# A two-layer decoder trunk: the down-projection of two SwiGLU blocks regrouped, with some additions moved from VectorE to GpSimd

## The chip, the cores and the metric

The kernel runs on one core of one Trainium2 chip. The metric is the device time of one execution in microseconds, as the median of several runs. Engines are named as in the profile: PE is TensorE (matmuls), PEld its weight loads, DVE is VectorE, ACT is ScalarE, POOL is GpSimd and SP is SyncE, which here only issues DMAs.

## What is computed

Two layers. Each layer adds half a SwiGLU to the residual, then a mixing part (attention beside a short convolution), then half of a second SwiGLU. There are therefore four SwiGLUs; the change touches the second (end of layer 0) and the third (start of layer 1) in all its parts, and the first and fourth in one.

```python
D_MODEL = 1024; SEQ = 512; DEPTH = 2; D_FF = 2816
def rms_norm(x, gain):
    inv = lax.rsqrt(jnp.mean(xf * xf, axis=-1, keepdims=True) + NORM_EPS)
    return (xf * inv).astype(x.dtype) * gain
def swiglu(h, w_gate, w_up, w_down):
    return (jax.nn.silu(h @ w_gate) * (h @ w_up)) @ w_down
for l in range(DEPTH):
    x = x + 0.5 * swiglu(rms_norm(x, ffn1_norm[l]), ffn1_wg[l], ffn1_wu[l], ffn1_wd[l])
    ...
    x = x + 0.5 * swiglu(rms_norm(x, ffn2_norm[l]), ffn2_wg[l], ffn2_wu[l], ffn2_wd[l])
return rms_norm(x, final_norm)
```

All data are float32. Every product is made of three matmuls: both factors are split into a rounded high part and a remainder (names ending in h and l), and high by high, high by low and low by high are added up in PSUM.

## The kernel before

The residual x stays in SBUF, features on partitions, as eight tiles of 128 x 512 (`xs[c]`, in pairs `xpair[m]`). The 2816 hidden columns of a SwiGLU are eleven blocks of 256, numbered 0 to 10. A table of stages gives the order of one SwiGLU (`INNER`, L33; `LAST`, L37, for the fourth). Its letters:

- **p**: gate and up of block 0, four groups of 24 matmuls. While they run, the norm's factor `inv` is found from the sum of squares (`factors`, L516, two matmuls in the second group), the normalized input is written in full (`scale`, L532, eight DVE operations named hf) and the first operand of the next stage is made (`make("b11")`).
- **d (0,)**: the part of the down-projection that belongs to block 0, 48 matmuls, added to x column by column (`down`, L343; L1249).
- **w b**: gate and up of blocks b and b+1 as a 2x2 block product with seven products in place of eight (Winograd's form), `winograd2`, L971. Each of the seven steps has two weight groups of 12 matmuls. The operands of the seven steps are b11, b21, t2, t3, t1, t4 and b22; t3 = b12 - b22, t2 = t3 - b11, t1 = b11 - b12 and t4 = t2 + b21 are sums of quarters of the input (`Seven.make`, L555), each 128 x 1024, and each operand is then split (ACT for the high part, DVE for the low part). They are made once, before and during the first w stage, and kept.
- **s b**: the down-projection of the four blocks from b on, again with seven products (`share`, L832), 168 matmuls. Its result is token-major; the `Apart` class keeps four quarters (o, t), sends them through DMA transposes (`send`, L892) and adds them to x (`back`, L902; one quarter goes through PE transposes).
- **d (9, 10)**: the part of blocks 9 and 10, 96 matmuls, with the last quarters added and, for each finished column c, `after(c)` (class `into`, L1672): the next norm's input split (`take`, L449: ACT and DVE) and the square added to the running sum nacc (`square`, L460: ACT, then a DVE addition at L467).
- **e 5** (fourth SwiGLU only): blocks 5 to 10 in one group with seven products of three weight groups each, 252 matmuls.

Weights come from HBM in pieces of 512 KB into eight buffers (`raw`); a sum of two weight blocks is made by a second, accumulating DMA that POOL issues (L220). Every weight group is then split into wh and wl (`need_split`, L233), three buffers of each, always two groups ahead of its use (`SPLIT_AHEAD`, L65). Normally ACT makes wh and DVE wl (L225). A group marked "far" spares DVE: ACT writes the negated weights to wl, and a DMA that POOL issues adds the raw weights to it (`split_far`, L227, L231). For a group marked "share" the sum of the weight blocks a12 and a11 is made by a DMA (L282) in place of a DVE addition (L284).

The framework orders each engine's instructions by their place in the program and by the buffers that come free, and sets the semaphores. Each engine, and each queue of DMA issues, then runs in that fixed order: an instruction that waits holds back those behind it.

Of the kernel before, what the change touches and what calls it, by code (L numbers as in the profile page):

```python
# [16 lines left out]
P = 128  # L17
# [19 lines left out]
LAST = INNER[:-2] + (("e", 5),)  # L37
FORMS = ("a11", "a12", "s2", "s3", "s1", "a22", "s4")
# [13 lines left out]
SENT_AT = {3: (0, 0), 4: (1, 1), 5: (1, 0)}  # L52
BACK_AT = {4: ((0, 0), (0, 1)), 5: ((1, 0),)}
# [21 lines left out]
def trunk_kernel(  # L75
# [29 lines left out]
    work = ctx.enter_context(tc.tile_pool(name="work", bufs=1))  # L105
    ps = ctx.enter_context(tc.tile_pool(name="ps", bufs=1, space=bass.MemoryType.PSUM))
# [126 lines left out]
    def need_split(g):  # L233
        while state["split"] <= min(g, len(order) - 1):
# [16 lines left out]
            elif isinstance(what, tuple):  # L251
# [4 lines left out]
                need_raw(u + h if far else u + max(last, 4) + h + LOAD_AHEAD)  # L256
# [33 lines left out]
            if far:  # L290

                with tc.issue_after(sent.ins):
                    need_raw(u + LOAD_AHEAD + (4 + h if isinstance(order[n][1], tuple) else 0))
# [62 lines left out]

    def plan():
# [19 lines left out]
        def ffn(wg, wu, wd, stages, near=False):  # L377
            for what, b in stages:
                how = "far" if b == (0,) and not near else None
                if what == "p":  # L380
                    plain(wg, wu, b)
                if what == "w":
                    seven(
                        lambda o, j, h: ((wg, wu)[o], KC // 2 * j + 2 * h, 2, 2 * b * P, S),
                        lambda what, h: "far" if (b, what, h) == (1, "a11", 0) else None,
# [6 lines left out]
                if what == "d":  # L392
                    cols(wd, 2 * b[0], 2 * len(b), KC, how, len(b) == 2)
# [14 lines left out]
        for l in range(DEPTH):  # L408
            ffn(ffn1_wg[l], ffn1_wu[l], ffn1_wd[l], INNER, l == 0)
# [7 lines left out]
            ffn(ffn2_wg[l], ffn2_wu[l], ffn2_wd[l], INNER if l + 1 < DEPTH else LAST)  # L417
# [18 lines left out]
    class Norm:  # L436
        def __init__(self, i):
# [5 lines left out]
            self.seven = Seven(self.full, room_g8, f"{i}")  # L443
# [16 lines left out]
        def square(self, c):  # L460
# [6 lines left out]
            nc.vector.tensor_add(self.acc, self.acc, sq)  # L467
# [78 lines left out]
    class Seven:  # L546
# [3 lines left out]
        def __init__(self, full, room, name, far=()):  # L550

            self.full, self.room, self.name, self.forms = full, room, name, {}
            self.far = far

        def make(self, *names):  # L555
            for what in names:
# [15 lines left out]
                if self.room is None:  # L572
# [7 lines left out]
                    if what == "t4":  # L580
                        nc.vector.tensor_add(b21, b11, b21)
# [295 lines left out]
    class Apart:  # L877
# [24 lines left out]
        def back(self, o, t):  # L902
# [824 lines left out]
```

## Time and profile before

| what | value |
|---|---|
| median of 3 runs | 1632.73 us (1632.26 to 1633.55) |
| the profiled execution | 1633.73 us, of which its span (first to last instruction) is 1631.9 us |
| PE matmuls | 7572, busy 1619.6 us |
| DVE, ACT, POOL busy | 1369.1, 1178.7, 223.5 us |
| read from HBM | 264.29 MB |

The profile is of one execution. Its parts are the busy time of each engine, the DMA queues, the chain of work that ended last (followed back from the last instruction), groups of instructions by line, and DMA issues. Further views of the same trace give the waits, the busy time of every engine in chosen stretches, and the instructions in order of time. A row of the timeline begins with its start and its length in us; consecutive matmuls overlap, so that their spacing, and not their length, is what each one costs. The second SwiGLU runs from 497 us to 820 us of the span, the third from 820 us to 1144 us.

### The profile page before, as it was taken

What the parts mean: (1) busy time and instruction counts of PE and PEld (TensorE: products, weight loads), DVE (VectorE), ACT (ScalarE), POOL (GpSimd) and SP (SyncE); (2) the same over time, 40 slices, a digit from 0 to 9 for tenths busy, and PEclk for the clock granted to TensorE, in tenths of its full rate; (3) what the DMA queues carried; (4) which work ended last, traced back from release to release, by engine and by line L of the source; (5) the groups of instructions that cost most, each with busy time, mean ns of one, the idle gap of its engine ahead of it and who ended that gap; (6) DMA issues with size and microseconds to landing.
All of it is one profiled execution on the core that took longest, in us unless ns stands there. A gap on an engine that the chain in (4) does not pass through costs nothing.

```text
span 1631.9 us, 21170 instructions
## 1 busy us (share of the span) xinstructions
PE 1619.6 (99%) x7572; PEld 1348.3 (83%) x7572; DVE 1369.1 (84%) x1779; ACT 1178.7 (72%) x1510; POOL 223.5 (14%) x199
## 2 busy tenths in 40 slices
PE   9999999999999999999999999999999999999998
PEld 6788888888898888888888888888888988888887
DVE  7978798888899877797998777979788998677997
ACT  6667778867766577777865777788586767878665
POOL 1211111001121111111011111110012111111121
PEclk9999999999999999999999999999999999999999
DMA  9899989922497699999966999999136978999992
GB/s 271 194 230 221 215 203 234 251 65 74 125 240 176 175 218 218 214 209 240 229 154 173 227 214 221 199 246 228 52 91 156 227 153 213 222 222 229 230 264 70
DMA packets 307166, 318.12 MB, mean 195 GB/s; under 512 B 125612, under 2 KB 188660, under 8 KB 307060
## 3 DMA queue, kind: packets, MB, share of 16 engines
q1 hardware_dynamic: 265140, 230.63, 49.9%
q0 software_dynamic: 41200, 85.47, 30.9%
q8 instruction: 59, 0.97, 0.2%
q10 hardware_dynamic: 720, 0.66, 0.1%
q14 instruction: 47, 0.39, 0.1%
HBM read 264.29 MB, written 2.10 MB: 163 GB/s over the span
## 4 chain that ended last, share of the span: by engine, by line
PE 89%; DVE 5%; ACT 3%; DMA 1%; issue 1%; SPq 0%; ACTq 0%; DVEq 0%
PE x L823 26%; PE y L823 13%; PE x_s L823 8%; PE w L823 6%; PE acc L311 6%; PE acc L312 6%; PE acc L314 6%; PE y_s L823 5%; PE x_m L808 3%; PE w_s L823 2%; PE y_m L808 1%; DVE wl L225 1%; PE y_e L823 1%; PE acc L685 1%; PE x_e L823 1%
## 5 line engine op out<-in xcount | busy, mean ns | idle before, releaser
L225 DVE TENSOR_TENSOR wl<-raw,wh 128x1024 fp32r<-128x1024 f32 (+1 forms) x493 | 598.4, 1221 | 172.6 <-ACT wh L225 171.7
L225 ACT CAST wh<-raw 128x1024 fp32r<-128x1024 f32 (+1 forms) x493 | 513.1, 1045 | 296.1 <-PE x L823 95.0
L311 PE MATMUL acc<-xh,wh 128*128 128x512 f32 x392 | 153.1, 392 | 0.5 <-ACT wh L225 0.5
L312 PE MATMUL acc<-xl,wh 128*128 128x512 f32 x392 | 153.4, 391 | 0.0
L314 PE MATMUL acc<-xh,wl 128*128 128x512 f32 x384 | 149.8, 390 | 0.0
L220 POOL DMA_DIRECT2D raw<-in_ffn_wu_dram x40 | 50.2, 1263 | 384.6 <-DMA raw<-in_ffn_wu_dram 311.2
L311 PEld LDWEIGHTS acc<-xh,wh 128*128 128x128 f32 x392 | 73.8, 188 | 15.1 <-ACT wh L225 0.6
L312 PEld LDWEIGHTS acc<-xl,wh 128*128 128x128 f32 x392 | 73.7, 188 | 15.0 <-DVE xl L458 0.5
L314 PEld LDWEIGHTS acc<-xh,wl 128*128 128x128 f32 x384 | 72.2, 188 | 15.0
L220 POOL DMA_DIRECT2D raw<-in_ffn_wg_dram x40 | 48.4, 1232 | 201.9 <-DMA raw<-in_ffn_wu_dram 104.7
L220 POOL DMA_DIRECT2D raw<-in_ffn_wd_dram x34 | 41.1, 1218 | 254.5 <-DMA raw<-in_ffn_wd_dram 99.9
L264 DVE TENSOR_TENSOR raw<-raw,raw 128x1024 f32<-128x1024 f32 x58 | 70.5, 1219 | 6.2 <-DMA raw<-in_ffn_wu_dram 4.7
L1085 ACT COPY raw_a<-turned 128x1024 uint16<-128x1024 uint16 x48 | 63.5, 1355 | 0.0
L823 PE MATMUL x<-wl,ft2h 128*128 128x512 f32 x160 | 62.2, 390 | 1.1 <-DVE wl L225 1.1
L823 PE MATMUL w<-wl,fb21h 128*128 128x512 f32 x160 | 62.4, 390 | 0.6 <-DVE wl L225 0.6
L823 PE MATMUL y<-wh,ft4h 128*128 128x512 f32 x160 | 62.4, 390 | 0.1
L823 PE MATMUL w<-wh,fb21h 128*128 128x512 f32 x160 | 62.4, 390 | 0.0
L823 PE MATMUL y<-wh,ft3h 128*128 128x512 f32 x160 | 62.3, 390 | 0.0
L823 PE MATMUL x<-wh,ft2h 128*128 128x512 f32 x160 | 62.3, 389 | 0.0
L823 PE MATMUL x<-wh,ft1h 128*128 128x512 f32 x160 | 62.3, 389 | 0.0
L823 PE MATMUL x<-wh,ft2l 128*128 128x512 f32 x160 | 62.3, 389 | 0.0
L823 PE MATMUL w<-wh,fb21l 128*128 128x512 f32 x160 | 62.3, 389 | 0.0
(506 smaller groups left out, 4544.2 us busy)
## 6 DMA issues: line engine op xcount, KB each, us to landing
raw<-in_ffn_wu_dram SPq DMA_DIRECT2D x127, 512.0 KB, 5.6
raw<-in_ffn_wd_dram SPq DMA_DIRECT2D x105, 512.0 KB, 5.7
raw<-in_ffn_wg_dram SPq DMA_DIRECT2D x86, 512.0 KB, 5.5
raw<-in_ffn_wu_dram POOLq DMA_DIRECT2D x40, 512.0 KB, 9.1
raw<-in_ffn_wg_dram POOLq DMA_DIRECT2D x40, 512.0 KB, 6.3
raw<-in_w_in_dram SPq DMA_DIRECT2D x36, 512.0 KB, 4.1
raw<-in_ffn_wd_dram POOLq DMA_DIRECT2D x34, 512.0 KB, 9.8
raw<-raw POOLq DMA_DIRECT2D x21, 512.0 KB, 8.2
```

The lines of the kernel that those rows point to most:

```text
L220: nc.gpsimd.dma_start(out=r, in_=rows_of(*more), accum_op=ALU.add)
L225: return nc.scalar.copy(hi, raw), eng.tensor_sub(lo, raw, f32(hi))
L264: nc.vector.tensor_add(a11, a11, s1)
L311: nc.tensor.matmul(acc, hi[:, k, :], rhs[k][0], start=k == first, stop=False)
L312: nc.tensor.matmul(acc, hi[:, k, :], rhs[k][1], start=False, stop=False)
L314: nc.tensor.matmul(acc, lo[:, k, :], rhs[k][0], start=False, stop=k == last)
L685: nc.tensor.matmul(opening[n], (lo if part == "w" else hi)[:, k, :], xl if part == "x" else xh, start=n not in begun, stop=k == KC - 1 and ...
L808: nc.tensor.matmul(accs[c // 2][:, c % 2, :], w[:, k, cols], x_[:, 2 * h + k, :], start=start and c % 2 == 0 and h + k + i == 0, stop=h + ...
L823: nc.tensor.matmul(accs[u], x_[:, 2 * h + k, tok], w[:, k, :], start=start and h + k + i == 0, stop=h + k == 2 and i == 2, skip_group_chec ...
L1085: nc.scalar.copy(words(raws[self.b][:, c, :]), self.to[:, :, c, :])
```

## The change

A new table of stages, `LATER`, takes the place of `INNER` for the second and third SwiGLU. In it:

- block 0's part of the down-projection moves from behind p to the very end. Its activation is not split at once; it is stored to DRAM by two DMAs on SP (`stay`), fetched back during the e stage (`bring`), and split there with the subtraction on GpSimd;
- w 1 follows p directly. Three of its first weight groups (a11 first half, a12 both halves) are "far", and the s3 sums are made by DMA; the operands are made two steps ahead of their use;
- s 5 and d (9, 10) become one e 5 group for blocks 5 to 10 (new function `six`), whose first operands are made during s 1. Two quarters of s 1's result are added to x in this stage, on GpSimd; the other two in the final d (0,).

In these two SwiGLUs the squares of the next norm are added on GpSimd. In all four SwiGLUs the sums t3, t2, t1 and t4 of the input are made on GpSimd (`adder`), and so are those of the e group in the second and third, but for t1.

```diff
+LATER = (
+    ("p", 0), ("w", 1), ("w", 3), ("w", 5), ("w", 7), ("w", 9), ("s", 1), ("e", 5), ("d", (0,)),
+)
+AHEAD = {4: ((0, ("b11",)),), 5: ((0, ("t2",)), (1, ("b11",))), 6: ((1, ("t2",)),)}
+SHARE_SENT_AT = {3: (1, 1), 4: (0, 0), 5: (1, 0)}
+SHARE_BACK_AT = {4: (1, 1), 6: (0, 0)}
+LATE_BACK_AT = {4: ((1, 0),), 5: ((0, 1),)}
+    away = ctx.enter_context(tc.tile_pool(name="away", bufs=1, space=bass.MemoryType.DRAM))
...
-                need_raw(u + h if far else u + max(last, 4) + h + LOAD_AHEAD)
+                need_raw(u + last + h if far else u + max(last, 4) + h + LOAD_AHEAD)
...
+    def first_how(what, h):
+        return {("a11", 0): "far", ("a12", 0): "far", ("a12", 1): "far"}.get(
+            (what, h), "share" if what == "s3" else None
+        )
...
         for l in range(DEPTH):
-            ffn(ffn1_wg[l], ffn1_wu[l], ffn1_wd[l], INNER, l == 0)
+            ffn(ffn1_wg[l], ffn1_wu[l], ffn1_wd[l], LATER if l else INNER, l == 0)
...
-            ffn(ffn2_wg[l], ffn2_wu[l], ffn2_wd[l], INNER if l + 1 < DEPTH else LAST)
+            ffn(ffn2_wg[l], ffn2_wu[l], ffn2_wd[l], LATER if l + 1 < DEPTH else LAST)
...
-            self.seven = Seven(self.full, room_g8, f"{i}")
+            self.seven = Seven(self.full, room_g8, f"{i}", adder=nc.gpsimd)
...
-            nc.vector.tensor_add(self.acc, self.acc, sq)
+            (nc.gpsimd if soft else nc.vector).tensor_add(self.acc, self.acc, sq)
...
                 if what == "t2":
                     self.sums = self.room(self.name)
                     t3, t2 = self.sums
-                    nc.vector.tensor_sub(t3, b12, b22)
-                    nc.vector.tensor_sub(t2, t3, b11)
+                    self.adder.tensor_sub(t3, b12, b22)
+                    self.adder.tensor_sub(t2, t3, b11)
                 if what == "t1":
-                    nc.vector.tensor_sub(b12, b11, b12)
+                    self.adder.tensor_sub(b12, b11, b12)
                 if what == "t4":
-                    nc.vector.tensor_add(self.sums[1], self.sums[1], b21)
+                    self.adder.tensor_add(self.sums[1], self.sums[1], b21)
...
+    def six(ops, accs, y, between):
+
+        for step, (acc, operand, (o, t, sign)) in enumerate(END):
+            start = acc not in accs
...
+            for n, op in enumerate(ops):
+                op.make(operand)
+                xh, xl = op.forms[operand]
+                for h in range(xh.shape[1] // 2):
+                    _, wh, wl = take_split()
+                    stream(accs[acc], wh, wl, xh, xl, h, start and n == 0)
+                if step + 1 < len(END):
+                    op.make(END[step + 1][1])
+            for u in range(2):
+                y.add(2 * t + u, o, accs[acc][u], 0.5 * sign)
+            between(step)
...
             def up(j, acc):
                 t = gates[j]
                 nc.vector.tensor_mul(t, acc, t)
-                split(hi[:, j, :], lo[:, j, :], t)
+                if delay:
+                    nc.sync.dma_start(out=stay[:, j, :], in_=t)
+                else:
+                    split(hi[:, j, :], lo[:, j, :], t)
...
                 norm.make("b11")
                 up(1, accs[3])
+                if delay:
+                    norm.make("b21")
...
-                if step < 3:
+                if delay and step < 5:
+                    norm.make(CHAINS[step + 2][1])
+                elif step < 3:
                     norm.make(CHAINS[step + 4][1])
...
+                def between(step):
+                    if step == 1:
+                        acts[0] = bring(acts[0])
+                    if step == 5:
+                        part = acts[0]
...
+                        split(hi, lo, part, nc.gpsimd)
+                    if step in SHARE_BACK_AT:
+                        apart.back(*SHARE_BACK_AT[step], nc.gpsimd)
+                    if step in SHARE_SENT_AT:
+                        apart.send(*SHARE_SENT_AT[step])
+
+                six(ends, kept, apart, between)
...
-                    for quarter in BACK_AT.get(c, ()):
+                    for quarter in (LATE_BACK_AT if delay else BACK_AT).get(c, ()):
...
-        ffn(norm, INNER, into(n1), None if l else bias_steps())
+        ffn(norm, LATER if l else INNER, into(n1, l > 0), None if l else bias_steps())
...
-            ffn(n2, INNER, into(n3))
+            ffn(n2, LATER, into(n3, True))
```

More of the change, by code (lines that the diff above doesn't have):

```diff
@@ L925, in back, with bring @@
                 nc.vector.tensor_add(part, part, tp)
+    def six(ops, accs, y, between):
+        for step, (acc, operand, (o, t, sign)) in enumerate(END):
+            start = acc not in accs
+            if start:
+                tag = {"x": "mm", "y": "sc", "w": "aux"}[acc]
+                accs[acc] = [psum(tag, [P, S], f"{acc}_{ops[0].name}_{u}") for u in range(2)]
+            for n, op in enumerate(ops):
[9 more added lines that the diff above has]
+            between(step)
+    def bring(stay):
+        part = form(f"near_{state['group']}", F32, (P, 2, S))
+        nc.sync.dma_start(out=part, in_=stay)
+        return part
     def ahead(ops, at):
@@ L1188, in ffn @@
                 winograd2(b, between)
-            if what == "s" and end:
+            if what == "s" and delay:
+                tail = crossing[-1]
+                ends = [
+                    Seven(lambda: [raws[5], raws[7]], None, f"e_{norm.i}_0", adder=nc.gpsimd),
+                    Seven(
+                        lambda: [tail.whole[:, j] for j in range(2)], None, f"e_{norm.i}_1", adder=nc.gpsimd
+                    ),
+                ]
+                share(
+                    ops,
+                    0.5,
+                    joined(lambda n: [ends[j].make(*what) for j, what in AHEAD.get(n, ())]),
+                    apart,
+                    still=kept,
+                )
+            elif what == "e" and delay:
+                def between(step):
[3 more added lines that the diff above has]
+                        part = acts[0]
+                        hi, lo = acts[0] = [
+                            form(f"a{n}_{norm.i}_0", shape=(P, 2, S)) for n in "hl"
+                        ]
+                        split(hi, lo, part, nc.gpsimd)
[4 more added lines that the diff above has]
+                six(ends, kept, apart, between)
+            elif what == "s" and end:
                 ends = [
```

48 lines of the change are left out of this document (29 added, 19 removed).

## The prediction

> **What bounds the kernel now.** The first part of the page and the sums of the chain that ended last say which engine sets the time:
>
> ```profile
> PE 1619.6 (99%) x7572; PEld 1348.3 (83%) x7572; DVE 1369.1 (84%) x1779; ACT 1178.7 (72%) x1510; POOL 223.5 (14%) x199
> PE 89%; DVE 5%; ACT 3%; DMA 1%; issue 1%; SPq 0%; ACTq 0%; DVEq 0%
> ```
>
> PE, without a break. What one matmul costs is read from the chain in order of time, where 24 matmuls make one step of a w stage; what PE waits for, from its waits over the whole span (the matmul rows among them):
>
> ```profile
> 612.10 5.44 PE w L823 x24
> 617.53 5.44 PE x L823 x24
> ...
> PE x L823 <- DVE wl L225: 1.1, 1, 1.1
> ...
> PE w L823 <- DVE wl L225: 0.6, 1, 0.6
> ```
>
> A step is 5.44 us, a matmul 5.44/24 = 0.227 us, and all the weights that came late cost 1.7 us. So the time is a count of matmuls plus a few stalls, and the question about any edit is whether PE still never waits. That hangs on the engine that feeds it, so next I read the busy times by stretch (columns: length; then busy us of PE, PEld, DVE, ACT, POOL; clock; DMA share; GB/s):
>
> ```profile
> 34.00:72.00 38.00, 36.87 (x161) 29.68 (x161) 37.72 (x39) 27.30 (x36) 10.35 (x11) 1.00 0.83 190
> 1317.00:1352.00 35.00, 35.00 (x160) 29.03 (x159) 34.40 (x41) 24.96 (x31) 5.44 (x5) 1.00 0.73 146
> 509.00:555.00 46.00, 46.00 (x205) 37.98 (x204) 45.11 (x52) 31.33 (x37) 7.54 (x7) 1.00 0.68 154
> 759.00:797.50 38.50, 38.37 (x168) 30.93 (x168) 35.52 (x37) 28.34 (x29) 4.20 (x4) 1.00 0.99 222
> 797.50:820.00 22.50, 22.50 (x105) 18.74 (x104) 21.04 (x31) 18.60 (x22) 0.00 (x0) 1.00 0.69 190
> 892.00:930.00 38.00, 38.00 (x169) 31.46 (x168) 27.61 (x29) 26.87 (x32) 5.42 (x5) 1.00 0.93 224
> ```
>
> In a plain w stage (892) DVE has 10 us of 38 free. In three kinds of stretch it has next to none: the openings of the SwiGLUs (34, 509, 1317: gates, normalized input, operands, w 1), s 5 (759), and the last stage d (9, 10) with the next norm's work (797.5). There PE is fed just in time. The change works on all of these.
>
> **The change, part by part.**
>
> *Fewer matmuls.* s 5 (168), d (9, 10) (96) become e 5 (252); p, w, s 1 and d (0,) keep theirs. 12 fewer in each of two SwiGLUs, 24 x 0.227 = **-5.4 us**. This part is certain, since PE is the bound in both stages.
>
> *s 5 against e 5.* In s 5 168 matmuls take 38.1 us and the stretch is 38.5: 0.4 us is lost there, twice. The e stage of the fourth SwiGLU shows what a group of this form costs:
>
> ```profile
> 1566.00:1624.00 58.00, 57.92 (x268) 47.99 (x267) 54.00 (x72) 34.37 (x49) 11.58 (x8) 1.00 0.54 129
> ```
>
> PE is busy throughout, with DMAs at 0.54, so the three more weight pieces (21 loads and sums in place of 18) are covered by free DMA time. If that cover were gone, three pieces at the stretch's 0.5 MB in about 2.4 us (222 GB/s above) would be 7 us, of which prefetch hides most. DVE is at 54 of 58, and GpSimd's own additions here (quarters, block 0's split) are new; I take 0.2 us lost in place of 0.4, **-0.4 us** for both (-0.8 to +4).
>
> *w 1 right behind p.* In the old order block 0's part, 11 us of PE, lay between p and w 1. These rows are the end of p and the preparation of a far group in the second SwiGLU (PE, ACT, POOL, DVE; then two far DMAs with their us to landing, and the summary of all of L231):
>
> ```profile
> 519.11 0.40 PE L314 MATMUL acc<-xh,wl 128*128 128x512 f32 x1
> 519.35 0.40 PE L330 MATMUL acc<-a,wh 128*128 128x512 f32 x1
> 519.54 1.06 ACT L229 ACTIVATE wl<-raw 128x1024 fp32r<-128x1024 f32 x1 [0.47 <-PE acc L314]
> 520.91 0.90 POOL L231 DMA_DIRECT2D wl<-raw  x1 [2.55 <-DVE a L225]
> 517.39 0.68 DVE L949 TENSOR_TENSOR gate<-acc,gate 128x512 f32<-128x512 f32 x1
> 517.99 1.22 DVE L225 TENSOR_TENSOR fb11l<-hf,fb11h 128x1024 fp32r<-128x1024 f32 x1
> ...
> wl<-raw POOLq DMA_DIRECT2D x1, 512.0 KB, 8.4
> wl<-raw POOLq DMA_DIRECT2D x1, 512.0 KB, 4.5
> DMA to landing us min/median/max: 4.4/7.7/9.1
> ```
>
> The buffer for a group comes free when the group three before it is done. At 519.35 p's last group ends, ACT negates until 520.6, the DMA is issued at 520.91, and lands 8.4 us later. In the old order that group is w 1's first, 10.9 us away: enough. In the new order the group in this very place is a12's first half, and only two groups of 12 lie before it: it is due at 519.35 + 5.44 + 0.45 (third matmul) = 525.2. With the median landing of 7.7 us it comes at 528.6, **3.4 us late**; with 4.5 (the other row, the first far copy during p) at 525.4, 0.2 late. At this place the row is 8.4, and w 1's other pieces are still loading in the new order too. I take 3.4. Queued behind this DMA on POOL are the second half's DMA and the sums t3 and t2; if a sum goes first, the DMA is later by up to 2.6 us, so 0.2 to 6. Beside it, fb11l ended at 519.2 for a PE that now needs it at 519.6. One more weight split (1.2 us) now stands before it on DVE and GpSimd's t3 runs beside it; up to 3 us, but the copy's clock starts at p's end, so this hides inside the 3.4. The two stores on SP hold back loads by at most an `up` multiplication (0.7 us), which eight buffers cover; the fetch back, one 512 KB DMA, has four e steps (over 30 us) before its use. Two SwiGLUs: **+6.8 us**.
>
> *Block 0's part last.* The old last stage, DVE operations from 797.7 to 827.1, and what waits for them at its end:
>
> ```profile
> L225 DVE TENSOR_TENSOR wl<-raw,wh 128x1024 fp32r<-128x1024 f32 x6 | 7.3, 1216 | 0.4 <-ACT wh L225 0.4
> L458 DVE SCALAR_TENSOR_TENSOR xl<-x,par,xh 128x512 fp32r<-128x512 f32 x8 | 5.9, 742 | 0.0
> L1249 DVE SCALAR_TENSOR_TENSOR x<-acc,x 128x512 f32<-128x512 f32 x8 | 5.3, 680 | 0.0
> L467 DVE TENSOR_TENSOR nacc<-nacc,nsq 128x512 f32<-128x512 f32 x7 | 4.8, 680 | 0.0
> L914 DVE TENSOR_TENSOR x<-x,back 128x512 f32<-128x512 f32 x6 | 4.0, 689 | 1.2 <-ACT back L910 1.2
> L890 DVE SCALAR_TENSOR_TENSOR apart<-x_s,apart 128x512 f32<-128x512 f32 x2 | 1.3, 680 | 0.0
> L925 DVE TENSOR_TENSOR x<-x,back 128x512 f32<-128x512 f32 x2 | 1.3, 678 | 0.0
> ...
> 825.00 0.68 DVE L467 TENSOR_TENSOR nacc<-nacc,nsq 128x512 f32<-128x512 f32 x1
> 826.37 0.69 DVE L225 TENSOR_TENSOR sql<-nacc,sqh 128x512 fp32r<-128x512 f32 x1 [0.69 <-ACT sqh L225]
> 827.17 0.39 PE L522 MATMUL ssq<-sqh,ones_r 128*128 128x512 f32 x1
> ```
>
> sql ends at 827.06 and PE takes the sum of squares at 827.17 and 227 ns later: no slack. The new last stage has half the matmuls. DVE must still do all evictions (8), input splits (8), apart additions (2), four of the eight quarter additions, and three weight splits: 5.3 + 5.9 + 1.3 + 1.3 + 1.3 + 3.7 = 18.8 us, less 0.08 us by which neighbours overlap, 26 times: 16.7, and about 1 us until the first group is done: 17.7. From the last split to sql the old order takes 2.1 us; with a GpSimd addition of 1.3 us (row below) in place of 0.68 it is 2.7, so 20.4 us from the stage's start. PE gets there after 48 + 24 + 6 matmuls and eight transposes (0.9 us): 18.6. **1.8 us late**, with no contention. The covers that go: the 10.9 us of matmuls under which this work lay. In return the squares (4.2 us) and two quarters leave DVE, counted above.
>
> *GpSimd's additions.* What such an addition takes, and what it does to DVE, from the convolution (POOL, then DVE):
>
> ```profile
> 403.84 1.29 POOL L1657 TENSOR_TENSOR cc<-cc,tap 128x511 f32<-128x511 f32 x1 [4.79 <-issue]
> 442.53 2.15 POOL L1658 TENSOR_TENSOR cc<-cc,inv 128x512 f32<-128x512 f32 x1
> 442.14 3.62 DVE L225 TENSOR_TENSOR wl<-raw,wh 128x1024 fp32r<-128x1024 f32 x2
> 405.21 1.64 POOL L1658 TENSOR_TENSOR cc<-cc,inv 128x512 f32<-128x512 f32 x1
> 406.15 0.34 DVE L1508 CUSTOM_DVE_ANT_0 p<-sc,bias,sink 128x128 f32<-128x128 f32 x1
> 406.42 0.97 DVE L1572 TENSOR_TENSOR pl<-crossing,ph 128x512 fp32r<-128x512 f32 x1
> ```
>
> Undisturbed 1.29 us for 512 columns; I take 2.6 for 1024, as no row has one. Two weight splits that need 2.4 us took 3.6 beside one such addition; a DVE operation that reads PSUM (sc) keeps its 0.34 us. So DVE's operations with two SBUF inputs stand still meanwhile: moving an addition of 1.14 us to GpSimd can cost DVE 2.6 us.
>
> [...]
>
> In the last stages seven squares hold GpSimd for 9.0 us, and 10.9 of DVE's 18.8 us have two SBUF inputs: at most 9.0 x 0.58 = 5.2 us are lost. I take 1.2, since many fall into waits: last stage 1.8 + 1.2 = 3.0 (0 to 7), twice: **+6.0 us**. In the openings of the first and fourth SwiGLU, with DVE at 37.72 of 38 and 34.40 of 35, four sums cost DVE 10.4 us in place of 4.6: at most +5.8. From below, -1.7: the late weights could vanish. In the first, where PE already waits, I take half, +3.0; in the fourth +1.5: **+4.5 us**. In the second and third the sums lie under the 3.4.
>
> Sum: -5.4 - 0.4 + 6.8 + 6.0 + 4.5 = +11.5. On the profiled execution (1633.7: span 1631.9, and 1.8 around it) this gives 1645.2; the median of the runs is 1.0 lower: **1644 us**.
>
> **The rivals.**
>
> *All covers hold: faster.* GpSimd works in DVE's PSUM operations, the far copies land in under 4.5 us because block 0's weights no longer load beside them, and DVE is ahead when the last stage begins. Then -5.4 - 0.4 and up to -1.7 remain: 1625 to 1627. The deciding point is the landing of the a12 copy: 4.3 us after issue is in time. For it: DVE is spared two splits, two sums and eight evictions in w 1; 4.5 us occurs. Against: the median landing is 7.7 us, and the old last stage ended without slack.
>
> *A wash.* One of the two large terms is real and the other hidden, GpSimd's sums cost nothing: -5.8 + 6 to 6.8, about 1633.
>
> *GpSimd and DVE exclude each other fully.* Sixteen sums at 2.6 - 1.14 = 1.5 us, 23 us; the last stages 2 x (1.8 + 5.2) = 14; the far copies hide behind that: 1632.7 - 5.8 + 37 = 1664, if no wait absorbs any.
>
> **How the numbers follow.** Forecast 0.50, full exclusion 0.12, wash 0.13, all covers 0.25. Slower by over 0.2% (3.3 us, about what a measurement of this kernel can tell from none) has the first two: 0.62; same 0.13; faster 0.25. For the forecast alone the terms' ends give 1634 to 1656. The range takes in the faster case and part of the full exclusion: 1625 to 1660.
>
> **What would show it.** 24 fewer matmuls, whatever the time. In the second and third SwiGLU a gap of PE after p's 96 matmuls and two groups, ended by a DMA into wl; a gap at ssq one group after the last stage, ended by DVE sql; in the opening of the first more than the 1.7 us of waits for wl; DVE's weight splits at over 2 us beside L588 to L593 on POOL. I am wrong if PE runs through these places without a gap, which means that the landing or the last stage's DVE sum was mis-sized.

## The result: 69 us slower, and the profile after

The changed kernel takes 1702.11 us (median of 4 runs, 1697.39 to 1706.72), the kernel before, run beside it, 1633.14 us (1632.26 to 1634.55). The ratio is 1.0421, 95% interval 1.0390 to 1.0453. The prediction, 1644 us with a range of 1625 to 1660, had the sign and missed the size: +11 forecast, +69 measured.

One sentence ahead of the prediction has to be corrected: in the e group of the second and third SwiGLU only t4 (L597 of the changed kernel) is made on GpSimd. t2, t3 (L590, L591) and t1 (L593) stay on VectorE there. No number of the prediction rests on it.

The first part of the page of the changed kernel:

```profile
PE 1641.0 (96%) x7548; PEld 1352.1 (79%) x7548; DVE 1393.5 (82%) x1739; ACT 1189.0 (70%) x1524; POOL 324.6 (19%) x253
```

PE has the 24 matmuls fewer, is busy for 21 us more, and no longer fills the span: 96% in place of 99%. DVE has 40 instructions fewer and is busy for 24 us more; that is the first sign that its instructions themselves became longer. What PE waits for (us in total, times, longest):

```profile
PE w L839 <- DMA wl<-raw: 8.0, 3, 4.3
PE y_e L839 <- ACT wh L233: 7.5, 2, 4.4
PE acc L319 <- DVE x L1336: 7.4, 4, 2.8
PE acc L320 <- DVE xl L473: 5.7, 5, 2.0
PE w L839 <- DVE wl L233: 5.6, 1, 5.6
PE x_e L839 <- DVE apart L906: 3.1, 4, 1.0
...
PE x L839 <- DVE fb11l L233: 2.4, 2, 1.2
...
PE w L839 <- ACT fb21h L233: 1.4, 1, 1.4
```

Before, the waits for weights came to 1.7 us. Now there is no one wait but a dozen kinds: in w 1 (w), in the e stage (x_e, y_e) and in the last stage (acc). The stretches show where they lie (the columns as before the change: length; then busy us of PE, PEld, DVE, ACT and POOL, each with its count of instructions; clock; DMA share; GB/s):

```profile
34.00:72.00 38.00, 30.91 (x123) 24.28 (x122) 37.75 (x30) 22.50 (x31) 20.86 (x15) 0.87 0.68 141
526.00:550.00 24.00, 17.61 (x62) 13.14 (x61) 22.68 (x17) 13.14 (x15) 15.60 (x8) 0.86 0.56 119
758.00:790.00 32.00, 28.71 (x119) 21.30 (x118) 29.07 (x32) 22.68 (x25) 8.93 (x8) 1.00 1.13 259
800.00:832.00 32.00, 26.86 (x108) 20.54 (x107) 22.66 (x21) 20.46 (x22) 8.30 (x5) 0.95 0.67 166
840.00:868.00 28.00, 21.54 (x87) 16.17 (x86) 25.40 (x26) 17.73 (x25) 13.68 (x9) 0.94 0.46 102
1375.00:1410.00 35.00, 31.90 (x128) 25.49 (x127) 32.05 (x36) 20.15 (x23) 18.00 (x11) 0.90 0.73 150
```

In the first of these stretches, 38 us in the opening of the first SwiGLU, PE did 123 matmuls where it had done 161: 38 x 0.227 = 8.6 us lost, in a stage in which nothing was changed but the engine of four sums. The others are w 1, the opening and the later part of the e stage, the last stage (all second SwiGLU) and the opening of the fourth. Summing over each place what the distance from one matmul's start to the next exceeds 0.227 us by, in the timeline of PE (in us):

| place | before | after | e1: all on VectorE | e15: e1 with two edits |
|---|---|---|---|---|
| opening of the first SwiGLU | 1.4 | 10.5 | 1.4 | 1.4 |
| w 1, second and third | 0 | 17.9 | 8.4 | 4.5 |
| e 5 (before: s 5), second and third | 1.5 | 24.2 | 12.8 | 7.0 |
| last stage and the next p, second and third | 0 | 18.9 | 6.5 | 6.5 |
| opening of the fourth | 0 | 6.3 | 0 | 0 |
| sum, less before's 2.9 and 5.4 for 24 matmuls | | +69.5 | +20.8 | +11.1 |
| measured against before | | +69.0 | +21.0 | +11.7 |

The two kernels of the last columns are experiments told below. The sums, each from one profiled execution, account for the measured times, so the question is what caused each row.

### The profile page after: what moved, and what is told of

The parts are those of the page before. It is cut to its first block, busy times and chain, and to the rows that moved or that the text cites. A ratio compares the mean times of both kernels' runs of the same rounds, so it can differ in the third digit from the quotient of the medians.

```text
span 1702.0 us, 21189 instructions
## 1 busy us (share of the span) xinstructions
PE 1641.0 (96%) x7548; PEld 1352.1 (79%) x7548; DVE 1393.5 (82%) x1739; ACT 1189.0 (70%) x1524; POOL 324.6 (19%) x253
## 5 line engine op out<-in xcount | busy, mean ns | idle before, releaser
L233 DVE TENSOR_TENSOR wl<-raw,wh 128x1024 fp32r<-128x1024 f32 (+1 forms) x499 | 621.7, 1253 | 216.9 <-ACT wh L233 216.4
L233 ACT CAST wh<-raw 128x1024 fp32r<-128x1024 f32 (+1 forms) x499 | 519.1, 1045 | 329.5 <-PE x L839 92.9
L228 POOL DMA_DIRECT2D raw<-in_ffn_wd_dram x38 | 45.7, 1222 | 259.5 <-DMA raw<-in_ffn_wd_dram 101.4
L839 PE MATMUL w<-wl,fb21h 128*128 128x512 f32 x160 | 65.1, 408 | 13.7 <-DMA wl<-raw 8.0
L272 DVE TENSOR_TENSOR raw<-raw,raw 128x1024 f32<-128x1024 f32 x54 | 77.5, 1435 | 0.5
L839 PE MATMUL x<-wh,fb11l 128*128 128x512 f32 x160 | 63.2, 395 | 2.4 <-DVE fb11l L233 2.4
L839 PE MATMUL x<-wl,fb11h 128*128 128x512 f32 x160 | 62.8, 393 | 0.0
L839 PE MATMUL y<-wh,ft3l 128*128 128x512 f32 x160 | 62.2, 389 | 0.0
L839 PE MATMUL y<-wl,ft3h 128*128 128x512 f32 x160 | 62.2, 389 | 0.0
```

Of the source, the lines that this page charges most:

```text
L228: nc.gpsimd.dma_start(out=r, in_=rows_of(*more), accum_op=ALU.add)
L233: return nc.scalar.copy(hi, raw), eng.tensor_sub(lo, raw, f32(hi))
L272: nc.vector.tensor_add(a11, a11, s1)
L839: nc.tensor.matmul(accs[u], x_[:, 2 * h + k, tok], w[:, k, :], start=start and h + k + i == 0, stop=h + k == 2 and i == 2, skip_group_chec ...
```

## The experiments

Theory **G**: a GpSimd addition makes VectorE's operations with two SBUF inputs stand still, and this is most of the loss. Rival **R**: the regrouping itself starves PE, and GpSimd does little. All differences below are to the runs of the kernel before in the same comparison.

### e1: the regrouping alone, every addition on VectorE

```diff
-            self.seven = Seven(self.full, room_g8, f"{i}", adder=nc.gpsimd)
+            self.seven = Seven(self.full, room_g8, f"{i}")
-            (nc.gpsimd if soft else nc.vector).tensor_add(self.acc, self.acc, sq)
+            nc.vector.tensor_add(self.acc, self.acc, sq)
-                        split(hi, lo, part, nc.gpsimd)
+                        split(hi, lo, part)
-                        apart.back(*SHARE_BACK_AT[step], nc.gpsimd)
+                        apart.back(*SHARE_BACK_AT[step])
```

and no `adder` for the two parts of the e group either.

> The change with every addition on VectorE again: the four sums of the input, the e group's t4, block 0's subtraction, two quarters, the squares. The order of the stages is the changed one. Theory G (GpSimd additions stop VectorE's operations with two SBUF inputs; in the changed kernel such weight splits take 3.0 to 5.0 us beside them in place of 1.2): most of the 69 us go, 1635 to 1650 us. Rival R (the regrouping itself starves PE: w 1 behind p, block 0 last, the e stage): at least 1670 us.

Measured: 1655.25 us, +21.0; ratio 1.0128 (1.0099 to 1.0157). So GpSimd's additions are 48 of the 69 us, and the regrouping costs 21. Both theories hold a part, G the larger one, though its upper end was passed. The waits that remain without GpSimd:

```profile
PE acc L319 <- DVE x L1336: 5.3, 4, 1.4
PE w L839 <- ACT fb21h L233: 4.0, 2, 2.6
PE x_e L839 <- DVE wl L233: 3.2, 6, 1.0
PE x_e L839 <- DVE apart L906: 3.1, 4, 1.0
PE w L839 <- DMA wl<-raw: 1.4, 2, 0.7
```

### e2, e3: the input sums alone

e2 is the kernel before with its four input sums on GpSimd in all four SwiGLUs; e3 is the changed kernel with only these sums back on VectorE.

```diff
 e2, from the kernel before
-                    nc.vector.tensor_sub(t3, b12, b22)
-                    nc.vector.tensor_sub(t2, t3, b11)
+                    self.adder.tensor_sub(t3, b12, b22)
+                    self.adder.tensor_sub(t2, t3, b11)
...
 e3, from the changed kernel
-            self.seven = Seven(self.full, room_g8, f"{i}", adder=nc.gpsimd)
+            self.seven = Seven(self.full, room_g8, f"{i}")
```

> The kernel before, with nothing changed but that the four sums t3, t2, t1, t4 of the input are made on GpSimd in all four SwiGLUs. Theory G: each opening loses what the first and fourth lose in the changed kernel (8 and 6 us), so 1655 to 1665 us. Rival R: within 5 us of 1633.

> The changed kernel with only the four sums of the input back on VectorE; squares, quarters and the e group's additions stay on GpSimd. Theory G: the losses in the first and fourth opening vanish (8 and 6 us) and those at w 1 in the second and third (10 and 8 us) shrink to the late copy of about 3 us each: 1672 to 1680 us. Rival R: the second and third keep their 18 us: 1688 us or more.

Measured: e2 1661.84 us (two runs, 1657.38 and 1666.31), +27.6, ratio 1.0165 (1.0118 to 1.0212); e3 1673.25 us, +39.0, ratio 1.0234 (1.0199 to 1.0270), which is 30 below the changed kernel's +69. Put in or taken out, sixteen sums are worth 28 to 30 us, about 1.8 each. Both as G had them.

### e8: sums that nobody reads

Late results or a blocked engine? In e8 the kernel before keeps all sums on VectorE, and GpSimd makes extra ones of the same size, in quarters, whose results are not used.

```diff
+    def again(a, b):
+        for k in range(KC // 2):
+            nc.gpsimd.tensor_sub(spare, a[:, k, :], b[:, k, :])
...
                     nc.vector.tensor_sub(t2, t3, b11)
+                    again(b22, b11)
+                    again(b21, b11)
```

(and one beside t1 and t4 each)

> The kernel before with all its sums unchanged on VectorE, and beside each of the four in every SwiGLU an extra one on GpSimd of the same size (four subtractions of 256 columns), whose result nobody reads. No operand can come later because GpSimd is slow: what is lost is lost to VectorE standing still, or to DMAs that GpSimd issues later. Theory G: weight splits on VectorE beside them take over 2 us in place of 1.22, and the time is 1648 to 1665 us (moving the four sums gave 1662). Rival L (the sums cost time only since their results, at 2.4 to 3.4 us in place of 1.2, are late for the matmuls): 1633 to 1638 us.

Measured: 1661.44 us, +28.3, ratio 1.0179 (1.0158 to 1.0200): as much as moving the sums cost. No sum made by GpSimd is used here, so late sums are not the cause. What PE waits for:

```profile
PE x L836 <- DMA wl<-raw: 6.5, 3, 2.6
PE x L836 <- ACT wh L225: 4.2, 1, 4.2
PE x L836 <- DVE wl L225: 4.2, 4, 1.8
PE w L836 <- DVE wl L225: 3.1, 2, 2.3
```

The last three rows are what G says: VectorE's splits, and a cast of ScalarE that stands behind a weight sum of VectorE. The first row is another cost of GpSimd's sums. In the second, third and fourth opening the DMA of a far copy stands in GpSimd's queue behind eight subtractions, 11.6 us by an estimate (8 x 1.45, from twelve that take 17.4 us in the first opening). In the second it is issued only at 538.96:

```profile
538.96 0.89 POOL L231 DMA_DIRECT2D wl<-raw  x1
```

So up to 6.5 of e8's 28 us are a blocked queue and not a blocked VectorE. In e2, where the sums are moved, the wait for such a DMA is 1.0 us, so there it explains little. VectorE's and GpSimd's rows in the opening of the first SwiGLU:

```profile
57.00 1.75 DVE L600 TENSOR_TENSOR hf<-hf 128x1024 f32<-128x1024 f32 x1
58.68 1.75 DVE L225 TENSOR_TENSOR ft3l<-sums,ft3h 128x1024 fp32r<-128x1024 f32 x1
60.35 1.74 DVE L264 TENSOR_TENSOR raw<-raw,raw 128x1024 f32<-128x1024 f32 x1
```

```profile
53.20 9.47 POOL L550 TENSOR_TENSOR spare<-hf,hf 128x256 f32<-128x256 f32 x6
```

VectorE's instructions start every 1.67 us in place of every 1.14 (1216 ns less the overlap of 0.08, as in the prediction). GpSimd's row is of six subtractions in 9.47 us. The three that start at 49.84, 51.52 and 53.20 have the same step, 1.68 us, as VectorE's instructions at 48.61, 50.29 and 51.97; I read this as the two engines taking turns, one instruction each. With whole sums the turn is longer, 2.36 us. These are the rows of the changed kernel in w 1 of the second SwiGLU, POOL and then DVE:

```profile
528.67 2.36 POOL L604 TENSOR_TENSOR sums<-hf,hf 128x1024 f32<-128x1024 f32 x1 [6.02 <-DVE hf L552]
531.11 3.23 POOL L605 TENSOR_TENSOR sums<-sums,hf 128x1024 f32<-128x1024 f32 x1
534.30 3.39 POOL L607 TENSOR_TENSOR hf<-hf 128x1024 f32<-128x1024 f32 x1
537.63 0.91 POOL L239 DMA_DIRECT2D wl<-raw  x1
```

```profile
528.49 0.69 DVE L993 TENSOR_TENSOR gate<-acc,gate 128x512 f32<-128x512 f32 x1
529.09 3.02 DVE L233 TENSOR_TENSOR fb11l<-hf,fb11h 128x1024 fp32r<-128x1024 f32 x1
532.04 0.68 DVE L993 TENSOR_TENSOR gate<-acc,gate 128x512 f32<-128x512 f32 x1
532.64 2.78 DVE L233 TENSOR_TENSOR fb21l<-hf,fb21h 128x1024 fp32r<-128x1024 f32 x1
535.35 3.43 DVE L272 TENSOR_TENSOR raw<-raw,raw 128x1024 f32<-128x1024 f32 x1
538.70 1.21 DVE L233 TENSOR_TENSOR ft2l<-sums,ft2h 128x1024 fp32r<-128x1024 f32 x1
```

fb11l takes 3.02 us, in place of 1.21 in e1, and ends 1.1 us after L604, which ends at 531.0: by this reading it gets its turn only then. Then the sum behind it, L605, has to wait (3.23 in place of 2.36). The gate, which reads PSUM, keeps its 0.68 us amid all this. PE waits for fb11l in two places, 1.2 us each (above).

### e5, e4: the squares

```diff
 e5, from e1; e4 is the reverse, from the changed kernel
-            nc.vector.tensor_add(self.acc, self.acc, sq)
+            (nc.gpsimd if soft else nc.vector).tensor_add(self.acc, self.acc, sq)
```

> The kernel of e1 (every addition on VectorE, 1655.3 us) with one thing put back: the squares of the next norm are added on GpSimd in the last stage of the second and third SwiGLU. Theory G (a GpSimd addition makes VectorE's operations with two SBUF inputs stand still): the last stages, which lose 3.3 us each in e1, lose 8 to 9.5 each as in the changed kernel, and the clock is halved for one stretch of 3.4 us behind at least one of them: 1664 to 1670 us. Rival (the squares come late in the changed kernel only because everything before them is late; with the rest on VectorE they take seven additions off the engine that is short): last stages at 3.3 or less, 1651 to 1658 us.

> The changed kernel with only the squares of the next norm back on VectorE. The two last stages with the group behind them lose 9.4 us each in the changed kernel. Theory G: they fall to about 3 us each (the 1.8 us worked out without contention, and a gap's aftermath): 1686 to 1692 us. Rival R: the halved stage is the cause and VectorE has 4.2 us more to do, so no change or slower: 1702 us or more.

Measured: e5 1659.09 us, +25.9, ratio 1.0155 (1.0136 to 1.0173), 5 above e1; e4 1699.26 us, +65.1, ratio 1.0394 (1.0358 to 1.0429), 4 below the changed kernel. The intervals overlap in either pair, so each difference alone is not clear of noise. Both lie between the theories: the squares cost less than G had it, and e5 is a little above its rival. The profile says why. In e5's second SwiGLU, DVE beside the squares:

```profile
825.93 2.31 DVE L233 TENSOR_TENSOR wl<-raw,wh 128x1024 fp32r<-128x1024 f32 x1
828.16 1.75 DVE L473 SCALAR_TENSOR_TENSOR xl<-x,par,xh 128x512 fp32r<-128x512 f32 x1
...
833.98 0.68 DVE L1336 SCALAR_TENSOR_TENSOR x<-acc,x 128x512 f32<-128x512 f32 x1
```

GpSimd's squares run until 829.37 and from 831.93 to 839.12. The splits stand still as G has it (2.31 and 1.75 in place of 1.22 and 0.74), the eviction from PSUM at 833.98 does not (0.68), and the last stages lose 7.1 us each in place of 3.3. But w 1 of the third SwiGLU then loses 1.2 in place of 5.4: I read this as a PE that arrives there later and waits less for the same data. The seven additions moved off VectorE are not a gain in either kernel.

### e6, e7: the additions of the e stage, and what ScalarE waits for

e6 is e1 with block 0's split, two quarters and t4 of the e stage on GpSimd again. e7 is e6 with one quarter added a step later:

```diff
 e7, from e6
-SHARE_BACK_AT = {4: (1, 1), 6: (0, 0)}
+SHARE_BACK_AT = {5: (1, 1), 6: (0, 0)}
```

> The kernel of e1 with another thing put back: in the e stage of the second and third SwiGLU the subtraction of block 0's split, the additions of two quarters and the operands' t4 are made on GpSimd. In e1 these stages lose 7 and 6 us, in the changed kernel 13 and 11. Theory G: back to 12 and 10, and the wait of ScalarE's copy back<-turned with the gap of PE behind it comes again, 1662 to 1669 us. Rival (in the changed kernel the stage is late from what went before, its sums in w 1 above all): within 3 us of e1, 1652 to 1658 us.

> The kernel of e6_e_part_only with the first quarter added to x one step later, in step 5 in place of step 4, so that its DMA transposes, sent in step 3, have a whole step (8 us) more before ScalarE copies from them. It tells apart how the additions of the e part cost time. Theory Q (ScalarE's copy waits for the transposes and holds back the weight casts queued behind it): the gaps of 4.8 and 3.5 us of PE at this place go, and the halved clock behind them, 7 to 12 us less than e6_e_part_only. Theory G alone (the addition itself blocks VectorE, wherever it stands): within 3 us of e6_e_part_only.

Measured: e6 1667.69 us, +34.5, ratio 1.0214 (1.0187 to 1.0240), 13.5 above e1; e7 1658.77 us, +25.6, ratio 1.0161 (1.0135 to 1.0186), 9 below e6. The later part of the e stage loses 7.6 us in the second and 5.3 in the third SwiGLU of e6, and 1.5 in each of e7. So most of what these additions cost is not a blocked VectorE. ScalarE in e6, then in e1, at the same place of the second SwiGLU:

```profile
801.58 2.55 ACT L926 COPY back<-turned 128x1024 uint16<-128x1024 uint16 x2 [5.41 <-DMA turned<-halves]
803.99 1.98 ACT L148 COPY halves<-apart 128x1024 uint16<-128x1024 uint16 x2
805.88 2.93 ACT L233 CAST wh<-raw 128x1024 fp32r<-128x1024 f32 x3
```

```profile
798.01 2.57 ACT L926 COPY back<-turned 128x1024 uint16<-128x1024 uint16 x2 [4.23 <-DMA turned<-halves]
800.45 1.04 ACT L233 CAST wh<-raw 128x1024 fp32r<-128x1024 f32 x1
801.38 2.00 ACT L148 COPY halves<-apart 128x1024 uint16<-128x1024 uint16 x2
```

In both, the copy of the first quarter waits 4 to 5 us for transposes sent one step earlier. In e1 a weight cast comes right behind it; in e6 the two copies of the next `send` stand between, and the cast comes 4.3 us after the copy's start, not 2.4. Moving the additions to another engine had let the framework order ScalarE's queue differently. In the changed kernel the order is that of e6, the wait is 5.89 us, and PE stands for 4.4 us at this point ("y_e <- ACT wh" above). What the additions cost beside this, between e7 and e1, is +4.6, with intervals that overlap; and e7's profiled execution has a wait of 4.6 us in s 1 ("y_s <- ACT wh"), behind a late weight load, which e6 has not. I did not settle that rest.

### e9, e14: no far copies of a12

```diff
-        return {("a11", 0): "far", ("a12", 0): "far", ("a12", 1): "far"}.get(
+        return {("a11", 0): "far"}.get(
```

> The kernel of e1 (1655.3 us) with the two halves of a12 in w 1 of the second and third SwiGLU split on ScalarE and VectorE as usual, in place of the copy negated by ScalarE and added by a DMA. It tests the step of the prediction by which this copy comes 3.4 us late, twice. Theory P (that step is right): the two w 1 stages, which lose 2.9 and 5.4 us in e1, lose at most 1 and 2, 1647 to 1650 us. Theory A (what is late in e1 is mostly the operand fb21 on ScalarE; a weight that waits for a DMA is 1.4 us of its waits in all): ScalarE has one negation less ahead of it, VectorE two splits more, 1651 to 1656 us. Rival D (VectorE can't take the two splits): 1657 us or more.

> The changed kernel (1702 us) with all its additions on GpSimd, and with the two halves of a12 in w 1 split on ScalarE and VectorE as usual (the edit of e9). Theory F (a good part of the cost of GpSimd's sums in w 1 comes by its queue, in which the DMA of the far copy stands behind three sums; PE's waits for such a DMA are 8.0 us in the changed kernel, 1.4 us in e1): the w 1 stages, 10.3 and 7.6 us, lose 3 to 6 each, 1688 to 1693 us. Rival (VectorE standing still is what costs time there, and two more weight splits on it stand still as well): 1696 us or more.

Measured: e9 (from e1) 1650.51 us, +16.8, ratio 1.0096 (1.0075 to 1.0117); e14 (from the changed kernel) 1697.35 us, +64.9, ratio 1.0397 (1.0368 to 1.0426). Without the copies either kernel is 4 us faster, with intervals that overlap; e9 falls between its theories P and A. In e9 w 1 loses 5.7 us in place of e1's 8.4. In e14 it loses 17.8 in place of 17.9, and the gain lies in the e and the last stages, which the edit doesn't touch. So the DMA's place behind GpSimd's sums is not what made w 1 expensive, although the rows above show it issued at 537.63, three sums late, and theory F falls. In w 1 of e14 PE waits 2.9 us for casts of ScalarE behind a weight sum of VectorE ("x <- ACT wh"), and for VectorE's own split:

```profile
PE x L839 <- DVE wl L233: 3.1, 2, 1.5
```

### e10, e11, e12: operands and evictions of the e group reordered

```diff
 e10, from e1
-AHEAD = {4: ((0, ("b11",)),), 5: ((0, ("t2",)), (1, ("b11",))), 6: ((1, ("t2",)),)}
+AHEAD = {4: ((0, ("b11",)),), 5: ((0, ("t2",)), (1, ("b11",)))}
...
 e11, from e10 (e12 is e11 with the edit of e9)
+                if n == 1:
+                    for u in range(2):
+                        y.add(2 * t + u, o, accs[acc][u], 0.5 * sign)
                 if step + 1 < len(END):
                     op.make(END[step + 1][1])
-            for u in range(2):
-                y.add(2 * t + u, o, accs[acc][u], 0.5 * sign)
```

> The kernel of e1 with the second half of operand t2 of the e group made inside the e group, where it is needed, in place of the end of s 1 (one entry of the table AHEAD left out). In e1 VectorE stands 1.75 us ahead of its subtractions at L590, waiting for ScalarE's joined halves (raw_a), with the split of a weight group queued behind, and PE's first gap in the e stage (1.35 us) ends with that split. Theory Q (the queue behind the waiting subtraction is what starves PE): the openings of the two e stages lose 2.5 to 3.5 us each in place of 5.1, 1649 to 1652 us. Rival (PE waits since the x accumulators are used in two steps running and have to be read in between): 1654 to 1657 us.

> The kernel of e10 with each step's accumulators of the e group read (Apart.add) ahead of the next operand's split, not behind it. In e1 the reading starts 1.4 us behind the last matmul of the step at one place, since a sum and a split (1.2 us each) stand before it on VectorE. Theory X (the x accumulators, used in two steps running, are read late): 1.5 to 3 us less than e10 over both stages. Rival: within 1 us of e10, or slower, since the operand then comes later.

> The kernel of e11 with the edit of e9 as well: the regrouping with every addition on VectorE and the three stalls met so far taken out as far as these edits do. If each edit's saving stands by itself: 1655.3 less the savings of e9 and e11, 1642 to 1652 us. The kernel before, 1633 us, is reached only if the last stages (3.3 us each in e1) lose nothing either, which none of the edits touches; below 1640 us none of the theories has an explanation.

Measured: e10 1665.46 us, +31.8, ratio 1.0187 (1.0162 to 1.0212); e11 1664.63 us, +30.9, ratio 1.0184 (1.0162 to 1.0206); e12 1662.88 us, +29.2, ratio 1.0181 (1.0144 to 1.0217). My theory for the e stage fell: all three are slower than e1, e10 and e12 by more than any of their theories had, e11 as its rival had it, no better than e10. In the new order of VectorE's queue one weight split and one weight sum more stand ahead of the accumulators' reading, and PE waits for that. Writing the reading first (e11) didn't change it, 6.5 us again, since the framework orders the queue itself. e10's waits:

```profile
PE x_e L839 <- DVE apart L906: 6.5, 2, 3.3
...
PE y_e L839 <- ACT wh L233: 3.9, 2, 2.8
```

The second row is ScalarE's order of e6, come back although no addition is on GpSimd here: it hangs on the order, not on the engine.

### e13, e15, e16: the join earlier, the quarter later

e15 is e9 with the edit of e7. e13 is e9 with the last activation of the e group sent and joined one step earlier; e16 is e13 with the edit of e7.

```diff
 e13, from e9
-                if n == 1:
+                if n == 1 - delay:
...
-                for t in {1: (0, 1), 2: (2, 3)}.get(n, ()):
+                for t in {1: (0, 1), 2: (2, 3)}.get(n + delay, ()):
...
-                if n == 5:
+                if n == 5 - delay:
                     self.whole = g8(f"raw_a_{self.name}", F32, (P, 2, 2, S))
                     self.rejoin(0)
-                if n == 6 and delay:
+                if n == 5 and delay:
                     self.rejoin(1)
```

> The kernel of e9 (1650.5 us) with the turned activation of blocks 9 and 10 sent through the DMA transposes one step of s 1 earlier (after steps 0 and 1) and joined by ScalarE one step earlier (steps 4 and 5). Theory J (the e stage's opening starves since the second half of this activation is joined only as the stage begins, and VectorE's sums, and the splits queued behind them, wait for it): the openings of the two e stages, 4.3 and 5.7 us in e9, fall to 2 to 3 each, 1644 to 1648 us. Rival (what starves PE is the sum of VectorE's work in these 20 us, eight sums and operand splits beside the weights' and the evictions, whenever the data come): within 2 us of e9.

> The kernel of e9 (1650.5 us) with the first quarter added to x one step later (step 5 in place of 4). In e9 ScalarE waits 4.0 us for the transposes too, but a weight cast stands right behind the copy and PE loses only 1.6 and 1.1 us there. Theory Q (what is lost at this place is ScalarE's wait): those 2.7 us less, 1647 to 1649 us. Rival (VectorE then has the quarter's additions later, in a fuller place): 1650 us or more.

> The kernel of e13 (1660.1 us) with the first quarter added to x one step later. Theory Q: the gaps of 3.3 and some 2 us behind ScalarE's wait for the transposes go, with the halved clock behind the first: 1651 to 1654 us. If theory J (the e stage's opening starves for the late joined half) is right beside that, it comes below e15, 1643 to 1647 us; if VectorE's sum of work is what starves PE, it is at e15 or above.

Measured: e13 1660.08 us, +27.6, ratio 1.0159 (1.0133 to 1.0184), above both its theories; e15 1645.06 us, +11.7, ratio 1.0071 (1.0055 to 1.0088), below Q's range; e16 1652.09 us, +18.7, ratio 1.0114 (1.0095 to 1.0134). e15 confirms the wait of ScalarE: it takes 5 us off e9, more than the 2.7 lost at that place (the rest is in places that the edit doesn't touch: the openings of the e stages, 10.0 to 7.0, and w 1, 5.7 to 4.5), and the stretch in the later part of the e stage is full again (e1, then e15):

```profile
796.00:810.00 14.00, 12.85 (x55) 9.87 (x54) 8.35 (x10) 10.87 (x11) 0.00 (x0) 1.00 0.60 166
```

```profile
792.00:806.00 14.00, 14.00 (x63) 11.58 (x63) 10.07 (x13) 11.29 (x11) 0.00 (x0) 1.00 0.86 188
```

The earlier join costs 7 us (e16 against e15), so theory J falls: in e16 PE waits before the e stage already ("x_s <- ACT wh", 3.9 us), beside ScalarE's joining copies. What starves the opening of the e stage, 7.0 us over both in e15, was only moved or made larger by the edits of e10 to e13 and e16. That it is the sum of VectorE's and ScalarE's work in these 20 us is the reading left; it is argued, not shown. No kernel here beats the one before.

## Why the prediction was wrong, step by step

*Fewer matmuls, -5.4.* Right: 7548 in place of 7572.

*GpSimd's additions, +4.5.* **This is the step that failed.** The four sums per SwiGLU cost 28 us (e2), the e stage's additions 13 (e6; 9 of it by ScalarE's queue, e7) and the squares 4 to 5 (e4, e5), together about 46 of the 48 us between e1 and the changed kernel. The prediction had the mechanism and the rows for it (two splits taking 3.62 in place of 2.4 us), called the full exclusion a rival with a chance of 0.12, and then allowed the sums half of the possible 5.8 us in one opening, a quarter in another, and nothing in the second and third SwiGLU, "under the 3.4". Two errors are in this. Taking a half and a quarter of a bound had no row behind it: VectorE had no free time in these openings, and the splits that stand still there are those PE waits for next. The first opening lost 9.1 us more and the fourth 6.3, over the bound of 5.8; nearly 3 us of each are a halved clock (last section), so the waits alone make some 6.3 and 3.6. And in the second and third SwiGLU the sums did not hide under the late far copy: they delayed its DMA (8.0 us of waits for it, 1.4 in e1) and fb11l, which it was to cover (1.2 us twice). With the halved clock behind these waits w 1 went from 8.4 (e1) to 17.9, and e14 shows that it would have lost as much without the copies.

*s 5 against e 5, -0.4.* This failed too: the stage loses 11.3 us more with every addition on VectorE (12.8 less 1.5) and 22.7 more in the changed kernel. The reason given, that the fourth SwiGLU's e group runs without a gap, didn't carry over. There no quarter is sent through transposes and joined by ScalarE in the middle of the stage; here ScalarE's wait for them is worth 3 to 5 us (e15 against e9, at its place and in all), 9 where the cast stands at the wrong place (e7 against e6). The prediction worked out DVE and DMA time for this stage, and never followed ScalarE's queue.

*w 1 right behind p, +6.8.* The size came out near without GpSimd, 8.4 in e1, but by luck, since the cause was another. The DMA of the far copy, the term's whole reason, is 1.4 us of the waits. The larger part is the high part of operand fb21 on ScalarE ("w <- ACT fb21h", 4.0), which the prediction did not follow. It stands behind the two copies of a far group, but with the copies of a12 gone (e9) 3.2 of the 4.0 us are left, and ScalarE then begins it 0.8 and 0.0 us after VectorE has written the last normalized input. So what comes late is mostly that input.

*Block 0's part last, +6.0.* 3.6 of it without contention; e1 has 6.5, waiting for VectorE's evictions ("acc <- DVE x"), the engine named, at another of its instructions than sql. Contention was put at 2.4; by the times of e4 and e5 it is 4 to 5. The mechanism held, a VectorE that is late in a halved stage, but the size was put at about half: 6.0 for some 11.

*The rival of full exclusion, 1664.* Its price for sixteen sums, 23 us, was close to the 28. Its total came out low since it let the far copies hide behind the sums and gave the e stage nothing; the runs show that the costs, each measured by itself, nearly add up: 21.0 (e1) + 27.6 (e2) + 13.5 (e6) + 4.9 (e5) = 67.0 of 69.0.

## What to carry to other kernels

Here, with PE fed just in time, additions moved from VectorE to GpSimd were no relief: sixteen sums cost 28 us (e2). VectorE's splits there have two SBUF inputs, and by the rows of w 1 an addition of 1.1 us became a block of 2.36 us ahead of a split that PE waited for (3.02 us in place of 1.21). The DMAs that GpSimd issued stood behind such sums too, with up to 6.5 us of waits in e8. So before moving an addition, look at what VectorE does beside it and at what waits behind it on GpSimd. Follow the queue of every engine in a stage that is rebuilt, the one with spare time too: ScalarE had 30% to spare and still held PE up (4.4 us), since one copy waited 5.89 us for a transfer with a weight cast queued behind it. When an edit changes the order in which a framework queues instructions, compare that order before looking for a cause in the edit itself.

## What was not expected of the hardware

PE's granted clock fell from 1.00 to 0.50 behind short waits. The stretch that ends with PE's first two waits in w 1 of the changed kernel, the one behind it, and matmuls in the latter:

```profile
528.00:531.70 3.70, 1.49 (x6) 0.67 (x4) 3.70 (x3) 2.95 (x3) 2.95 (x2) 1.00 0.59 145
531.70:535.11 3.41, 2.94 (x7) 2.37 (x8) 3.41 (x3) 0.74 (x1) 3.41 (x2) 0.50 0.20 77
```

```profile
533.19 0.63 PE L839 MATMUL x<-wh,fb11h 128*128 128x512 f32 x1
533.62 0.63 PE L839 MATMUL x<-wh,fb11l 128*128 128x512 f32 x1
```

PE was busy for 1.49 of 3.70 us, with two gaps of about 1.8 us each from start to start; then the granted clock is 0.50 for 3.41 us, and matmuls start every 0.43 us in place of 0.227. A single wait of 2.58 us is followed by the same step of 0.43 us in e1, where the granted clock is 0.54 from 854 to 856:

```profile
854.05 0.73 PE L839 MATMUL w<-wh,fb21h 128*128 128x512 f32 x1 [2.58 <-ACT fb21h L233]
855.00 0.63 PE L839 MATMUL x<-wl,fb11h 128*128 128x512 f32 x1
855.43 0.63 PE L839 MATMUL x<-wh,fb11h 128*128 128x512 f32 x1
```

The length of a wait alone does not decide it. In the changed kernel two waits of 2.8 us in the last stages ("acc <- DVE x", ended at 853.66 and 1201.86) passed at full clock, 1.00 until 862.77 and 1210.92, while waits of 2.0 us after them ("acc <- DVE xl", ended at 862.44 and 1210.63) were each followed by 3.41 us at 0.50; in e15, with a wait of 1.9 us in w 1, the clock stays at 1.000 in the mean of the span. What decides is left open. In the changed kernel the clock was at 0.50 in nine stretches besides its end, seven of 3.4 us, one of 10.24 (53.81 to 64.05, in the first opening) and one of 6.83 (1391.83 to 1398.66, in the fourth), and some 70 matmuls were spaced by 0.43 us in them: by an estimate 70 x 0.2 = 14 of the 69 us, for which the prediction had no term; less, where PE would have waited for data anyway.
